# One encoder trunk on one core: the low part of each weight slab in four pieces

## The chip, the cores and the metric

The kernel runs on one core of a Trainium2 chip. A core has five engines with instruction queues of their own that meet through semaphores: TensorE (PE in the profile; its weight loads are shown as PEld), VectorE (DVE), ScalarE (ACT), GpSimd (POOL) and SyncE (SP), which here issues all DMA loads and stores. An engine takes its instructions in the order of its queue; one that waits holds up all behind it. The metric is the device time of one execution in microseconds, the median of several runs.

## The reference

The program is a hybrid encoder trunk of two layers over 1024 tokens and 1024 channels in float32. Each layer normalizes, modulates with shift and scale vectors that come from a conditioning vector, mixes, and adds the gated result to the stream:

```python
mod = c_act @ ada_w[l] + ada_b[l]
shift, scale, gate = jnp.split(mod, 3, axis=-1)
h = rms_norm(x, norm_g[l]) * (1.0 + scale[:, None, :]) + shift[:, None, :]
x = x + gate[:, None, :] * mixer(h)          # after both layers: rms_norm(x, final_g)
```

Layer 0's mixer projects `h @ w_in` into differential attention (4 heads, two softmax maps each) and a bidirectional gated linear recurrence, multiplies each by a SiLU gate and projects the pair with `w_out`. Layer 1's mixer is neighbourhood attention (16 heads on a 16 x 64 grid of tokens, 8 x 16 windows) with a SiLU gate, between two projections of the same kind.

## The kernel before

**Projections.** Activations stand channels by tokens in SBUF, split into eight row chunks of 128 channels (`KC = 8`) and two halves of 512 tokens (`HF`). Each projection works by weight slabs: a slab is 1024 input channels by 128 output channels, held as a tile of 128 partitions by 8 chunks by 128 columns. There are 80 slabs in one list: 24 of layer 0's input projection, 16 of its output projection (the same 8, once for each half of the tokens), 32 of layer 1's input and 8 of its output projection.

**Two-part products.** TensorE multiplies in a reduced float format (`F32R`). To keep float32 accuracy, every operand is split into a high part (the value rounded to that format) and a low part (the value minus the high part), and `mm3` (lines 203 to 206) issues three products for each chunk: high by high, high by the activation's low part, and the weight's low part by high. `proj` (line 245) runs the eight chunks of one slab over one half of the tokens, so 24 products into one PSUM bank; the low part of chunk k is first read by the third product of chunk k. In the value projection of layer 1 (`v1_job`) one slab holds four chunks of 256 columns.

**The supply of slabs.** `load_next` (line 152) issues the load of a raw slab (0.5 MB) on SP into one of two raw buffers. `split_next` (line 161) takes the next raw slab, lets ScalarE copy it into the high tile (line 187) and GpSimd subtract it into the low tile (line 188), and then issues the loads that may follow. A raw buffer is free for its next load when the slab's high and low parts are made; a high or low buffer is free when TensorE has read it. `ahead(i)` has a slab split while the one before is in use.

**What sets the order.** The kernel is recorded through a tile framework that tracks every tile's readers and writers, draws all semaphores, and orders each engine's queue itself by priorities and its own estimate of when things are ready; `high_priority` and `issue_after` bend that order in places. The two lines of the split are inside such a block.

**Stages.** At the start (0 to some 72 us) the first three slabs are multiplied chunk by chunk as the normalized activations come in (`products`, lines 573 to 575), while four groups of modulation sums (`mod_first`, line 281) arrive. Then come the recurrence (its scans and products on VectorE, `pair` and `evac_gb`, lines 743 to 822, with a small split of its own in `gate_w`, line 740), layer 0's attention (lines 982 to 1093; `head_norm` works by small dependent steps in `rstd_rows`, lines 388 to 394, on VectorE), the two output projections with layer 1's modulation sums woven in (`out_layer`, from line 1126; line 1160 sums squares for the next norm), layer 1's input projections and attention (`na_a`, `na_b`, `na_c`, lines 1360 to 1431; GpSimd scales the softmax rows at line 1389), and the last projection with the final norm.

Of the kernel before, what the change touches and what calls it, by code (L numbers as in the profile page):

```python
# [15 lines left out]
ALU = mybir.AluOpType  # L16
# [6 lines left out]
KC = 8  # L23
# [74 lines left out]
def kernel(ctx, tc, xT, xTp, small, lamp, adaw, tb, w0, gw, wo0, w1, nab, wo1, out):  # L98
    nc = tc.nc
    V, A, G, T = nc.vector, nc.scalar, nc.gpsimd, nc.tensor  # L100
# [51 lines left out]
    def load_next():  # L152
        i = state["load"]
        if i >= len(slabs):
            state["load"] = i + 1
            return
        raws[i] = wp.tile([P, KC, P], F32, tag="raw", name=f"raw{i}")
        nc.sync.dma_start(raws[i][:], slabs[i])
        state["load"] = i + 1

    def split_next():
        i = state["split"]
        if i >= len(slabs):
            return
        while state["load"] <= i:
            load_next()
        raw = raws.pop(i)
        pool = wp
        if state["third"] is not None:
            state["turn"] = (state["turn"] + 1) % 3  # L170
            pool = wp if state["turn"] else state["third"]
        tags = ("whi", "wlo")
        if i == 2:
            pool, tags = kqp, ("ks1", "ks1")
        if i == at1["g", 0]:
            pool, tags = mixp[1], ("mix6", "mix7")
        j = i - len(slabs) + KC
        if j >= 0:

            pool = (wp, kqp, mixa, mixp[1])[j // 2]  # L180
            if j >= 2:
                tags = (("ks0", "ks0"), ("ks1", "ks1"), ("mix0", "mix1"), ("mix2", "mix3"),
                        ("mix4", "mix5"), ("mix6", "mix7"))[j - 2]
        hi = pool.tile([P, KC, P], F32R, tag=tags[0], name=f"whi{i}")
        lo = pool.tile([P, KC, P], F32R, tag=tags[1], name=f"wlo{i}")
        with tc.high_priority() if j < 2 else tc.issue_after(state["pool"]):
            A.activation(hi[:], raw[:], AF.Copy)  # L187
            G.tensor_tensor(lo[:], raw[:], hi[:], ALU.subtract)  # L188
        ready[i] = (hi, lo)
        state["split"] = i + 1  # L190
        while state["load"] <= i + state["depth"]:
            load_next()

    def slab(i):
        while state["split"] <= i:
            split_next()
        return ready[i]

    def ahead(i):
        if state["split"] <= i:  # L200
            split_next()
# [423 lines left out]
    def evac_k(key):  # L625
        def f(hf, ps):
            if hf == 0 or (key, 0) not in ks_:
                ks_[key, 0] = kqp.tile([P, S], F32R, tag="ks0", name="ks0")
                ks_[key, 1] = kqp.tile([P, S], F32R, tag="ks1", name="ks1")
            def dst(t, b):  # L630
                x = t[b:b + 64, hf * HF:(hf + 1) * HF]
                return x if key[0] == "a" else by_tile(x)

            def src(b):
                x = ps[b:b + 64, :]
                return x if key[0] == "a" else x.rearrange("p (b g y) -> p b g y", g=2, b=4)

            k0, k1 = ks_[key, 0], ks_[key, 1]
            A.activation(dst(k0, 0), src(0), AF.Copy)
            A.activation(dst(k1, 64), src(64), AF.Copy)  # L640
            V.tensor_tensor(dst(k0, 64), src(0), dst(k0, 0), ALU.subtract)
            V.tensor_tensor(dst(k1, 0), src(64), dst(k1, 64), ALU.subtract)
        return f
# [261 lines left out]
    with ExitStack() as l0:  # L905
# [39 lines left out]
        for h in range(1, DA_HEADS):  # L945
            k = at0[c_k + h], evac_k(("a", h))
# [635 lines left out]
```

## Time and profile before

| | |
|---|---|
| three runs | 1188.19 us median (1186.65, 1188.19, 1191.43) |
| the profiled execution | 1190.72 us, span of its instructions 1189.0 us |
| busy: TensorE, VectorE, ScalarE, GpSimd | 1145.3, 738.1, 560.3, 371.8 us |
| the low parts (line 188) | 80 instructions, 197.0 us, 2465 ns each in the mean |
| the high parts (line 187) | 80 instructions, 84.3 us, 1056 ns each |
| TensorE's granted clock, mean | 0.989 |

The profile is one execution. Its page gives busy times, groups of instructions by source line, and for each group the idle time of the engine just ahead of it with what ended that idle time. Further views of the same trace are the waits by who waited for whom, a timeline of each engine (start, duration, line, operation, out<-in, and in brackets an idle time ahead and its releaser), statistics by line, and windows. Rows of "SPq" are DMA issues in SP's queue. A row with x2 or more merges instructions that follow each other. The durations on GpSimd are rougher than the others.

### The profile page before, as it was taken

To read this page: it belongs to the slowest core of one execution; us is meant where nothing else is said; L and a number is where in the kernel's file an instruction comes from. 1 tells how busy PE (TensorE), PEld (TensorE's weight loads), DVE (VectorE), ACT (ScalarE), POOL (GpSimd) and SP (SyncE) were. 2 spreads that over 40 slices of the span, in tenths; PEclk is the share of its full clock that TensorE was granted. 3 is DMA by queue.
4 is the path that set the end of the run, shared out by engine and by line. 5 is a ranking of instruction groups with operands and counts; after the bars stand their busy time and mean duration, and the time that the engine had idled before them with its cause. 6 is when DMAs were issued, how large, how long until landed. Compare 5 with 4: busy or idle time off the path is not lost.

```text
span 1189.0 us, 19211 instructions
## 1 busy us (share of the span) xinstructions
PE 1145.3 (96%) x7232; PEld 975.3 (82%) x7232; DVE 738.1 (62%) x1422; ACT 560.3 (47%) x1029; POOL 371.8 (31%) x346
## 2 busy tenths in 40 slices
PE   5999999999999999999999999999999999999997
PEld 2788777888887888777878888988998998888896
DVE  6857959699888979778663344233434443555454
ACT  4357685475655657432442444344444434446121
POOL 2124322233333332343422433332333333316100
PEclk8999999999999999999999999999999999999998
DMA  9723131432122112485513433243453534314212
GB/s 325 240 80 125 36 140 53 142 90 78 36 87 63 32 39 71 145 283 183 185 46 123 139 111 91 85 134 110 129 172 88 162 126 117 93 35 156 98 72 71
DMA packets 85789, 136.46 MB, mean 115 GB/s; under 512 B 8000, under 2 KB 49472, under 8 KB 85696
## 3 DMA queue, kind: packets, MB, share of 16 engines
q1 hardware_dynamic: 85696, 135.23, 36.3%
q8 instruction: 57, 0.93, 0.3%
q14 instruction: 36, 0.29, 0.1%
HBM read 112.13 MB, written 16.78 MB: 108 GB/s over the span
## 4 chain that ended last, share of the span: by engine, by line
PE 74%; DVE 13%; ACT 5%; DMA 4%; issue 3%; POOL 1%; SPq 0%; DVEq 0%; POOLq 0%; ACTq 0%
PE pp L204 14%; PE pp L205 14%; PE pp L206 14%; PE no L1418 4%; PE etr L1400 3%; PE v L204 2%; PE v L206 2%; PE v L205 2%; PE n L671 2%; DVE e L1003 2%; PE atr L1033 2%; PE n L672 2%; PE s L671 1%; PE s L672 1%; DMA ada<-in_adaw_dram 1%
## 5 line engine op out<-in xcount | busy, mean ns | idle before, releaser
L204 PE MATMUL pp<-ahi,whi 128*128 128x512 f32 (+1 forms) x976 | 370.8, 380 | 2.0 <-DVE sgb L677 1.8
L206 PE MATMUL pp<-ahi,wlo 128*128 128x512 f32 (+1 forms) x976 | 367.9, 377 | 1.1 <-POOL wlo L188 1.1
L205 PE MATMUL pp<-alo,whi 128*128 128x512 f32 (+1 forms) x976 | 368.6, 378 | 0.0
L188 POOL TENSOR_TENSOR wlo<-raw,whi 128x1024 fp32r<-128x1024 f32 x80 | 197.0, 2465 | 260.9 <-ACT whi L187 242.2
L206 PEld LDWEIGHTS pp<-ahi,wlo 128*128 128x128 f32 x976 | 184.0, 189 | 35.5 <-POOL wlo L188 1.6
L204 PEld LDWEIGHTS pp<-ahi,whi 128*128 128x128 f32 x976 | 184.3, 189 | 34.8 <-DVE sgb L677 2.3
L205 PEld LDWEIGHTS pp<-alo,whi 128*128 128x128 f32 x976 | 184.3, 189 | 30.8 <-issue 0.2
L1389 POOL TENSOR_SCALAR e<-e,r 128x288 f32<-128x288 f32 (+1 forms) x128 | 71.2, 569 | 235.9 <-DVE r L1387 229.7
L187 ACT ACTIVATE whi<-raw 128x1024 fp32r<-128x1024 f32 x80 | 84.3, 1056 | 107.1 <-PE pp L205 52.7
L1007 ACT ACTIVATE e<-e,nm 128x1024 f32<-128x1024 f32 x64 | 73.6, 1151 | 46.6 <-DVE nm L1003 46.3
L1384 ACT ACTIVATE e<-e,nm 128x288 f32<-128x288 f32 (+1 forms) x128 | 72.7, 569 | 47.2 <-DVE nm L1381 40.4
L1406 DVE COPY e<-etr 96x384 f32<-96x384 f32 (+1 forms) x64 | 35.5, 554 | 94.2 <-PE etr L1400 91.5
L1381 DVE CUSTOM_DVE_ANT_0 e<-n,bias 128x288 f32<-128x288 f32 (+1 forms) x128 | 60.6, 504 | 45.5 <-PE n L672 33.0
L1404 ACT ACTIVATE e<-etr 96x384 f32<-96x384 f32 (+1 forms) x64 | 31.3, 489 | 117.8 <-DVE e L1406 117.4
L1003 DVE CUSTOM_DVE_ANT_0 e<-s,tb 128x1024 f32<-128x1024 f32 x64 | 77.3, 1218 | 6.4 <-PE s L672 4.9
L1024 POOL TENSOR_SCALAR e<-e,r 128x256 f32<-128x256 f32 x32 | 32.6, 1018 | 131.8 <-DVE r L1013 73.7
L204 PE MATMUL v<-whi,ahi 128*128 128x256 f32 x256 | 72.2, 282 | 0.0
L206 PE MATMUL v<-whi,alo 128*128 128x256 f32 x256 | 71.9, 281 | 0.0
L205 PE MATMUL v<-wlo,ahi 128*128 128x256 f32 x256 | 71.9, 281 | 0.0
L1040 ACT ACTIVATE ath<-atr 128x512 fp32r<-128x512 f32 x64 | 37.5, 596 | 39.7 <-PE atr L1033 39.4
L1400 PE MATMUL etr<-ident,e 128*96 128x128 f32 (+1 forms) x384 | 52.3, 272 | 0.5 <-POOL e L1389 0.5
L671 PE MATMUL s<-ks,qq 128*128 128x512 f32 x128 | 52.5, 410 | 0.0
(218 smaller groups left out, 2111.3 us busy)
## 6 DMA issues: line engine op xcount, KB each, us to landing
raw<-in_w_dram SPq DMA_DIRECT2D x56, 512.0 KB
ada<-in_adaw_dram SPq DMA_DIRECT2D x96, 256.0 KB
raw<-in_wo_dram SPq DMA_DIRECT2D x24, 512.0 KB
bias<-in_nab_dram SPq DMA_DIRECT2D x64, 144.0 KB
qq<-qq SPq DMA_DIRECT2D x48, 128.0 KB
bias<-in_nab_dram SPq DMA_DIRECT2D x32, 192.0 KB
xT<-in_xT_dram SPq DMA_DIRECT2D x16, 256.0 KB
vd<-vt SPq DMA_DIRECT2D x32, 128.0 KB
```

What stands on the lines that cost most here:

```text
L187: A.activation(hi[:], raw[:], AF.Copy)
L188: G.tensor_tensor(lo[:], raw[:], hi[:], ALU.subtract)
L204: T.matmul(ps, lh, rh, start=start, stop=False)
L205: T.matmul(ps, lh, rl, start=False, stop=False)
L206: state["pe"] = T.matmul(ps, ll, rh, start=False, stop=stop).ins
L671: T.matmul(dst, qsel(q[m]), k, start=True, stop=False)
L1003: state["dve"] = V.tensor_tensor_reduce(out=e[:], in0=ps[:].rearrange("p a b -> p (a b)"), in1=tbt["tb"][:, o:o + S], scale=-1.0, scalar=3 ...
L1007: A.activation(e[:], e[:], AF.Exp, scale=-1.0, bias=nm[:], accum_out=sums[:, m:m + 1])
L1381: state["dve"] = V.tensor_tensor_reduce(out=e[:, m, :n], in0=ps[:, m, :n], in1=bias["now"][m][:, :n], scale=-1.0, scalar=3.0e38, op0=ALU.a ...
L1384: A.activation(e[:, m, :n], e[:, m, :n], AF.Exp, scale=-1.0, bias=nm[:, m:m + 1], accum_out=sums[:, m:m + 1])
L1389: state["pool"] = G.tensor_scalar(e[:, m, :n], e[:, m, :n], r[:, m:m + 1], 0.0, ALU.mult, ALU.add).ins
L1400: T.transpose(pt[:kn, m, j * P:(j + 1) * P], e[:, m, j * kn:(j + 1) * kn], ident[:])
```

## The change

The subtraction of line 188 is made by four instructions of two row chunks (256 columns) each instead of one of 1024 columns:

```diff
         with tc.high_priority() if j < 2 else tc.issue_after(state["pool"]):
             A.activation(hi[:], raw[:], AF.Copy)
-            G.tensor_tensor(lo[:], raw[:], hi[:], ALU.subtract)
+
+            for k in range(0, KC, 2):
+                G.tensor_tensor(lo[:, k:k + 2], raw[:, k:k + 2], hi[:, k:k + 2], ALU.subtract)
```

The high part stays one instruction on ScalarE, the loads stay whole slabs. Lines behind the change have numbers that are two higher in the changed program: the four pieces are line 190 there, `mm3`'s products 206 to 208.

GpSimd's queue at the end of layer 0, before and then with the change (`wlo40` is the low part of slab 40, the first of layer 1; `whi` the high part, `raw` the loaded slab):

```order
L188 TENSOR_TENSOR wlo40_5641<-raw40_5560,whi40_5640 128x1024
L188 TENSOR_TENSOR wlo42_5703<-raw42_5644,whi42_5702 128x1024
L188 TENSOR_TENSOR wlo41_5647<-raw41_5608,whi41_5646 128x1024
L188 TENSOR_TENSOR wlo43_5886<-raw43_5650,whi43_5885 128x1024
L188 TENSOR_TENSOR wlo44_5920<-raw44_5706,whi44_5919 128x1024
L188 TENSOR_TENSOR wlo45_6033<-raw45_5889,whi45_6032 128x1024
```

```order
L190 TENSOR_TENSOR wlo40_5761<-raw40_5677,whi40_5760 128x256 x4
L190 TENSOR_TENSOR wlo42_5829<-raw42_5767,whi42_5828 128x256 x4
L190 TENSOR_TENSOR wlo41_5770<-raw41_5728,whi41_5769 128x256 x4
L190 TENSOR_TENSOR wlo43_6015<-raw43_5776,whi43_6014 128x256 x4
L190 TENSOR_TENSOR wlo44_6052<-raw44_5835,whi44_6051 128x256 x4
L190 TENSOR_TENSOR wlo45_6168<-raw45_6021,whi45_6167 128x256 x4
```

The order of the slabs is kept (42 ahead of 41 in both), and the four pieces of a slab follow each other. Only in two slabs of the 80 something else of GpSimd's stands between the first piece and the other three: a memset of 64x512 in one, a step of a constant in the other.

TensorE's queue where slab 41 is first used, with the semaphores that each product waits for, before and then with the change (`ahi0` and `alo0` are the activation's parts of chunk 0):

```order
L204 MATMUL pp41_0_5708<-ahi0_0_5418,whi41_5646 128x512 [waits Activation_49]
L205 MATMUL pp41_0_5708<-alo0_0_5419,whi41_5646 128x512
L206 MATMUL pp41_0_5708<-ahi0_0_5418,wlo41_5647 128x512 [waits Pool_49]
L204 MATMUL pp41_0_5708<-ahi1_0_5423,whi41_5646 128x512
L205 MATMUL pp41_0_5708<-alo1_0_5424,whi41_5646 128x512
L206 MATMUL pp41_0_5708<-ahi1_0_5423,wlo41_5647 128x512
L204 MATMUL pp41_0_5708<-ahi2_0_5466,whi41_5646 128x512
L205 MATMUL pp41_0_5708<-alo2_0_5467,whi41_5646 128x512
L206 MATMUL pp41_0_5708<-ahi2_0_5466,wlo41_5647 128x512
```

```order
L206 MATMUL pp41_0_5837<-ahi0_0_5526,whi41_5769 128x512 [waits Activation_49]
L207 MATMUL pp41_0_5837<-alo0_0_5527,whi41_5769 128x512
L208 MATMUL pp41_0_5837<-ahi0_0_5526,wlo41_5770 128x512 [waits Pool_49]
L206 MATMUL pp41_0_5837<-ahi1_0_5531,whi41_5769 128x512
L207 MATMUL pp41_0_5837<-alo1_0_5532,whi41_5769 128x512
L208 MATMUL pp41_0_5837<-ahi1_0_5531,wlo41_5770 128x512
L206 MATMUL pp41_0_5837<-ahi2_0_5577,whi41_5769 128x512
L207 MATMUL pp41_0_5837<-alo2_0_5578,whi41_5769 128x512
L208 MATMUL pp41_0_5837<-ahi2_0_5577,wlo41_5770 128x512 [waits Pool_49]
```

The products stand in the same order. Before, the first product with the low part waits for the whole of it; now it waits for the piece of chunks 0 and 1, and the product of chunk 2 waits for the next piece. Over the program TensorE has 264 instructions that wait for GpSimd instead of 203.

TensorE's queue at the start, around the third group of modulation sums (`mod_500` before, `mod_509` with the change; `start` are the banks of the first three slabs):

```order
L575 MATMUL start_450<-alo_0_626,whi_295 128x512
L573 MATMUL start_669<-ahi_1_490,whi_464 128x512
L575 MATMUL start_556<-alo_1_491,whi_295 128x512
L573 MATMUL start_556<-ahi_1_495,whi_295 128x512
L574 MATMUL start_556<-ahi_1_495,wlo_296 128x512
L575 MATMUL start_556<-alo_1_496,whi_295 128x512
L281 MATMUL mod_500<-ada,c_126 32x128 x32
L575 MATMUL start_457<-alo_1_491,whi_388 128x512
```

```order
L575 MATMUL start_463<-ahi_1_499,whi_391 128x512
L283 MATMUL mod_509<-ada,c_126 32x128 x32
L577 MATMUL start_565<-alo_1_500,whi_295 128x512
L575 MATMUL start_565<-ahi_1_504,whi_295 128x512
L576 MATMUL start_565<-ahi_1_504,wlo_296 128x512
L308 MATMUL mod_509<-pick,mrow 128x4
L577 MATMUL start_565<-alo_1_505,whi_295 128x512
L576 MATMUL start_463<-ahi_1_499,wlo_392 128x512
```

The sums of the third group stand seven products earlier, those of the fourth likewise; a few steps of VectorE and ScalarE that belong to these groups move by one to three places. Behind the start the queues of TensorE, VectorE, ScalarE and SP are the same instruction by instruction.

## The prediction

> **What bounds the kernel now.** I read the page first: TensorE is the busy engine, and the instruction that the change cuts is GpSimd's largest group.
>
> ```profile
> PE 1145.3 (96%) x7232; PEld 975.3 (82%) x7232; DVE 738.1 (62%) x1422; ACT 560.3 (47%) x1029; POOL 371.8 (31%) x346
> L188 POOL TENSOR_TENSOR wlo<-raw,whi 128x1024 fp32r<-128x1024 f32 x80 | 197.0, 2465 | 260.9 <-ACT whi L187 242.2
> ```
>
> TensorE is idle for 1189.0 - 1145.3 = 43.7 us of the span; GpSimd works for 31% of it. So the time moves only where one of TensorE's few waits moves. The waits of TensorE by releaser are therefore the next view (us in total, times, longest).
>
> ```profile
> PE start L573 <- ACT ahi L415: 4.0, 2, 2.0
> PE obc L407 <- DVE osq L394: 2.3, 2, 2.0
> PE o L204 <- DVE atl L1041: 2.0, 2, 1.6
> PE n L671 <- DVE sg L677: 1.9, 1, 1.9
> PE pp L204 <- DVE sgb L677: 1.8, 1, 1.8
> PE pp L206 <- POOL wlo L188: 1.1, 1, 1.1
> ```
>
> In 80 slabs TensorE waits once for a low part, and for 1.1 us. The obvious gain, a first piece that is there early, is worth about that much. The other rows say where else to look: most of them end with VectorE. The statistics by line (min/median/max, ns) show that VectorE has something to do with the low parts:
>
> ```profile
> L188 POOL TENSOR_TENSOR wlo<-raw,whi x80: 2342/2402/3216, 6.4 to 1103.8; 128x1024 fp32r<-128x1024 f32 x80
> L1025 POOL TENSOR_TENSOR e<-e,e x32: 724/738/1387, 235.0 to 488.6; 128x256 f32<-128x256 f32 x32
> L1160 DVE TENSOR_TENSOR sq<-sq x34: 417/686/2765, 512.0 to 1175.9; 128x512 f32<-128x512 f32 x21, 128x256 f32<-128x256 f32 x13
> ```
>
> L1160, a sum of two SBUF tiles, takes 0.69 us in the median and up to 2.77. The timelines of layer 0's end show when (start, duration; `SPq` rows are DMA issues):
>
> ```profile
> 582.37 2.40 POOL L188 TENSOR_TENSOR wlo<-raw,whi 128x1024 fp32r<-128x1024 f32 x1 [3.03 <-ACT whi L187]
> 587.80 2.40 POOL L188 TENSOR_TENSOR wlo<-raw,whi 128x1024 fp32r<-128x1024 f32 x1 [3.04 <-ACT whi L187]
> 594.93 5.17 POOL L188 TENSOR_TENSOR wlo<-raw,whi 128x1024 fp32r<-128x1024 f32 x2 [4.73 <-ACT whi L187]
> ...
> 588.29 2.46 DVE L1160 TENSOR_TENSOR sq<-sq 128x512 f32<-128x512 f32 x1 [0.70 <-ACT sq L1154]
> 596.36 1.52 DVE L1160 TENSOR_TENSOR sq<-sq 128x512 f32<-128x512 f32 x1 [3.32 <-ACT sq L1154]
> ...
> 590.23 0.33 SPq L158 DMA_DIRECT2D raw<-in_w_dram  x1
> ...
> 593.79 2.01 ACT L187 ACTIVATE whi<-raw 128x1024 fp32r<-128x1024 f32 x2 [5.53 <-DMA raw<-in_w_dram]
> ```
>
> The sum that starts at 588.29 ends at 590.75, 0.55 us after the low part's end at 590.20: VectorE stands still while GpSimd's instruction runs. The pair at 594.93 shows who is next: the first low part ends about 597.33, the sum of 596.36 ends at 597.88, again 0.55 us later, though GpSimd's second instruction was already queued; and the pair takes 5.17 instead of 2 x 2.40 = 4.80, so the second one waited for VectorE. They alternate, one instruction each. This is what four pieces change.
>
> **The change, part by part.**
>
> *What GpSimd pays.* A two-input piece of 256 columns has a row of its own, L1025: 0.74 us. Four make 2.95 us, 0.55 more than 2.40, alone; 80 x 0.55 = 44 us on an engine with 1189.0 - 371.8 = 817 us idle, so nothing by itself. Below: the pieces stream with no cost each, 2.40; above: 4 x 1.387 = 5.5 us, the longest row. I take 0.55, since nearly all L1025 rows stand at the median. [...]
>
> *What VectorE gains.* An operation with two SBUF inputs that meets a low part now waits for one piece, at most 0.74 us, not for up to 2.4. But with four pieces queued, up to four of VectorE's operations in a row each wait for one: a dense run of them loses as much as before, only spread. A gain is left where fewer than four stand in the way. So I go to TensorE's waits one by one, with 0.74 us for each wait.
>
> A, the start:
>
> ```profile
> 21.88 2.81 POOL L188 TENSOR_TENSOR wlo<-raw,whi 128x1024 fp32r<-128x1024 f32 x1 [12.37 <-ACT whi L187]
> 21.72 3.52 DVE L414 SCALAR_TENSOR_TENSOR xT<-xT,gain,bcs 128x512 f32<-128x512 f32 x2
> ```
>
> Two operations of about 0.7 us take 3.52: about 2.1 us of waiting. With pieces the second ends about 1.4 us earlier; the next ones (L416, L535) then pay for the other pieces. Bounds -1.4 and +0.6 us (three more waits); I take -1.0, as TensorE waits for the first of them.
>
> B, layer 0's second group of gates (TensorE's 1.8 us wait for `sgb`):
>
> ```profile
> 200.40 2.69 POOL L188 TENSOR_TENSOR wlo<-raw,whi 128x1024 fp32r<-128x1024 f32 x1 [9.46 <-ACT whi L187]
> 200.93 3.24 DVE L798 TENSOR_TENSOR t<-t,w 128x1024 f32<-128x1024 f32 x1
> 204.09 0.68 DVE L677 SCALAR_TENSOR_TENSOR sgb<-sgb,pp 128x512 f32<-128x512 f32 x1
> ```
>
> One operation in the way, then L677, which takes its second input from PSUM. L798 is held for about 2.69 + 200.40 - 200.93 = 2.16 us; a piece holds it for 0.74: -1.4, and I take -1.5 of the 1.8 there (bounds 0 and -1.8).
>
> C, the head norm (TensorE's longest `osq` wait, 2.0 us):
>
> ```profile
> 374.66 2.79 POOL L188 TENSOR_TENSOR wlo<-raw,whi 128x1024 fp32r<-128x1024 f32 x1 [6.54 <-PE s L672]
> 375.13 2.47 DVE L394 SCALAR_TENSOR_TENSOR osq<-osq 128x128 f32<-128x128 f32 x1
> 378.29 0.29 DVE L394 SCALAR_TENSOR_TENSOR osq<-osq 128x128 f32<-128x128 f32 x1
> 378.60:383.00 4.40, 4.37 (x18) 4.10 (x19) 2.84 (x6) 0.60 (x1) 2.44 (x3) 0.61 0.45 140
> ```
>
> Here four small dependent operations follow each other (L394, L392, L393, L394), so each may meet a piece: 4 x 0.74 = 3.0 against 2.47 - 0.29 = 2.2 us now. If a piece only holds VectorE for the 0.55 us seen above, 2.2 as well, less what the first has already run. Bounds -0.7 and +0.8; I take -0.3.
>
> D, two gate products before the last head:
>
> ```profile
> 476.68 3.50 DVE L943 TENSOR_TENSOR vT<-vT,sga 128x512 f32<-128x512 f32 x2
> 480.10 1.28 DVE L1041 TENSOR_TENSOR atl<-atr,ath 128x512 fp32r<-128x512 f32 x2
> ```
>
> Two operations of 0.7 us take 3.50; with a wait of 0.74 each, 2.9: L1041, for which TensorE waits 1.6 us, comes 0.6 to 1.1 us earlier. I take -0.9.
>
> *What the finer wait gains.* F: the one wait of TensorE for a low part (1.1 us) is for the second of the pair at 594.93. Its first piece alone is wanted, but the chain in front of it gets longer: low part 587.80 (+0.55, and one wait of 0.55 for L1160), then the load that may only be issued when it has ended (590.23), then the copy on ScalarE (593.79), then the four pieces of the other slab. So: the last low part costs 0.74 where it cost 2.40 and 0.37 of waiting (5.17 - 4.80), -2.0; the chain ahead of it +0.55 + 0.55, and the other slab's pieces +0.55. That is -0.4 us; bounds -1.1 and +1.0.
>
> *What it costs.* G: a slab's raw buffer is free, and its next load issued from SP's queue, only when the last piece is done. This is covered nearly everywhere, but not at the entry to layer 1's attention:
>
> ```profile
> 622.30 4.76 POOL L188 TENSOR_TENSOR wlo<-raw,whi 128x1024 fp32r<-128x1024 f32 x2 [22.20 <-ACT whi L187]
> 624.73 0.33 SPq L158 DMA_DIRECT2D raw<-in_w_dram  x1
> 629.03 1.06 ACT L187 ACTIVATE whi<-raw 128x1024 fp32r<-128x1024 f32 x1 [3.53 <-DMA raw<-in_w_dram]
> 630.12 0.60 ACT L676 ACTIVATE sg<-pp 128x512 f32<-128x512 f32 x1
> 632.97 1.37 SPq L1357 DMA_DIRECT2D bias<-in_nab_dram  x3
> 641.21 0.56 DVE L1381 CUSTOM_DVE_ANT_0 e<-n,bias 128x384 f32<-128x384 f32 x1 [2.80 <-DMA bias<-in_nab_dram]
> 641.83 0.44 PE L671 MATMUL n<-ks,qq 128*128 128x384 f32 x1 [1.05 <-DVE nm L1381]
> ```
>
> The low part that starts at 622.30 frees the load of 624.73; its landing ends ScalarE's wait at 629.03; L676 is queued behind that copy, VectorE's `sg` behind L676, and TensorE's 1.9 us wait ends there. +0.55. The next low part, later by as much and longer by as much, holds SP's next weight load, and the bias loads at 632.97 are queued behind that; TensorE's 1.05 us wait at 641.83 ends with a bias: +0.55 again. Together +1.1 (bounds 0 and +2).
>
> *At nothing.* The 61 waits that TensorE gains for single pieces end long before it comes to them, apart from F. The sums of two modulation groups move seven matmuls forward on TensorE at the start; the same matmuls run, and if the loads are not there yet the wait is inside A's bounds. The memset that now stands behind the first piece of C's slab gives VectorE one more opening there, inside C's bounds.
>
> Sum: -1.0 - 1.5 - 0.3 - 0.9 - 0.4 + 1.1 = **-3.0 us**. The profiled execution took 1190.72 us (span 1189.0), so about 1187.7; the median of the three runs is 1188.19, 2.5 lower, and on it I forecast **1185.2 us**: 0.3% less, which is no change that can be measured. 0.5% is 5.9 us, about what a measurement of this kernel can tell.
>
> **The rivals.**
>
> *More comes back (faster).* The window quoted under C has a granted clock of 0.61 in the 4.4 us after that wait: 4.4 x 0.39 = 1.7 us lost besides the wait itself. If the wait shrinks and the clock stays up, if pieces hold VectorE for 0.55 rather than 0.74 (A -1.4, B -1.8, C -0.7, D -1.1) and if G is hidden, the sum is -1.4 - 1.8 - 0.7 - 1.7 - 1.1 - 1.1 = -7.8: **1180.4**. For it: the 0.55 was seen twice. Against: C has four operations in a row, and G's waits are real. [...]
>
> *Nothing but G (no change).* If GpSimd keeps its turn from piece to piece, VectorE waits as before and 0.55 us longer: +1.1, **1189.3**. The pair at 594.93 speaks against it, but those were two instructions with different waits, not four with none between them.
>
> *The supply runs late (slower).* Place: the out projection and layer 1's first slabs (about 500 to 600 us), where the low parts of 582.37 and 587.80 stand 5.43 us apart, so two raw buffers must turn round in 10.9. A slow load there takes
>
> ```profile
> 524.99 6.54 DMA raw<-in_wo_dram
> ```
>
> 6.54; with the copy (1.06) and the low part (2.40) that makes 10.0, and 0.9 is left. It decides from a low part of 3.3 us on, and 2.95 plus one wait of 0.55 for L1160 is 3.5. Then each of some seven turns costs 0.2 us or more, and each new TensorE wait can drop the clock as under C (1.7 us): 7 x 0.2 + 4 x 1.7 + G 1.1 = +9.3, **1197.5**. Against: most loads there take 3.5 us (590.23 to the copy at 593.79), and TensorE waits for no slab there ahead of the one at F.
>
> **How the numbers follow.** The forecast (-3.0, its own range 1182 to 1188) 0.46; more comes back 0.24; nothing but G 0.20; supply late 0.10. Low: 1180, the faster rival's number. High: 1191, that of the rival without a gain, with the 1.5 us by which the median stands above the fastest run. That leaves out the slower case and the fast half of the faster one. Faster by over 0.5% (below 1182.3): 0.24 from the one rival and 0.02 from the forecast's edge; slower (above 1194.1): 0.10; the rest, 0.64, is no change.
>
> **What would show it.** Right: GpSimd's line has 320 operations of about 0.74 us and busy time grows by some 45 us; L1160's longest falls from 2.77 to below 1.6; TensorE's waits for `sgb` near 204 and `o` near 480 shrink by about 1 us, those near 631 and 641 grow by 0.5 each. Wrong: VectorE's longest waits stay at 2.4 and more (GpSimd keeps its turn); pieces of 0.9 us and more; new TensorE waits on `wlo` or on `whi` between 500 and 600 (supply); a changed share of slow clock, which would outweigh the sum.

## The result and the profile after

The changed kernel took **1180.93 us** in the median of seven runs (1179.38 to 1184.22), the kernel before 1188.19 (1185.11 to 1191.43, seven runs): a ratio of 0.9942, 95% interval 0.9924 to 0.9959. Set against it again beside the last experiments, it came to 0.9958 (0.9946 to 0.9970). So it is faster by about half a per cent, 5 to 7 us; 3.0 us were forecast. The profiled execution took 1183.27 us (span 1181.5), 7.45 less than the one before.

The page after, engines and the group of the low parts:

```profile
PE 1142.2 (97%) x7232; PEld 974.7 (82%) x7232; DVE 715.9 (61%) x1422; ACT 559.5 (47%) x1029; POOL 440.5 (37%) x586
L190 POOL TENSOR_TENSOR wlo<-raw,whi 128x256 fp32r<-128x256 f32 x320 | 264.3, 859 | 221.0 <-ACT whi L187 199.0
```

GpSimd works 69 us more, VectorE 22 us less: the instructions of VectorE that stood still behind a low part stand still for less. TensorE's waits after (us in total, times, longest):

```profile
PE start L575 <- ACT ahi L417: 4.5, 2, 2.5
PE n L673 <- DVE sg L679: 2.8, 1, 2.8
PE obc L409 <- DVE osq L396: 1.3, 2, 0.8
PE o L206 <- DVE atl L1043: 0.9, 2, 0.6
```

The 1.8 us for `sgb` in `pp` are gone, the longest `osq` wait fell from 2.0 to 0.8, `atl` from 1.6 to 0.6; the wait for `sg` grew from 1.9 to 2.8. Two stretches of the trace say more than these totals.

**Behind slab 29, in the out projection.** Timeline before (GpSimd's low part of slab 29, VectorE, SP's issues, ScalarE, TensorE):

```profile
520.23 2.62 POOL L188 TENSOR_TENSOR wlo<-raw,whi 128x1024 fp32r<-128x1024 f32 x1 [4.48 <-ACT whi L187]
520.63 2.77 DVE L344 SCALAR_TENSOR_TENSOR macc<-ada,ctmp,macc 128x512 f32<-128x512 f32 x1
524.09 0.33 SPq L1152 DMA_DIRECT2D x1d<-xh  x1
524.46 0.44 SPq L330 DMA_DIRECT2D ada<-in_adaw_dram  x1
524.99 0.40 SPq L158 DMA_DIRECT2D raw<-in_wo_dram  x1
531.64 1.06 ACT L187 ACTIVATE whi<-raw 128x1024 fp32r<-128x1024 f32 x1 [4.86 <-DMA raw<-in_wo_dram]
532.91 0.59 PE L361 MATMUL mrow<-pick,macc 128*128 128x4 f32 x2 [2.75 <-ACT macc L356]
```

and the same in the timeline after:

```profile
514.85 3.39 POOL L190 TENSOR_TENSOR wlo<-raw,whi 128x256 fp32r<-128x256 f32 x4 [2.08 <-ACT whi L187]
514.34 1.90 DVE L346 SCALAR_TENSOR_TENSOR macc<-ada,ctmp,macc 128x512 f32<-128x512 f32 x2
518.27 0.33 SPq L158 DMA_DIRECT2D raw<-in_wo_dram  x1
525.08 1.06 ACT L187 ACTIVATE whi<-raw 128x1024 fp32r<-128x1024 f32 x1 [2.99 <-DMA raw<-in_wo_dram]
526.36 0.38 PE L363 MATMUL mrow<-pick,macc 128*128 128x4 f32 x2 [0.61 <-ACT macc L358]
```

What SP's queue waits for in this stretch, before (519.3 to 527 us) and then after (513 to 519), of the latter the wait of the load itself:

```profile
SPq L1152 <- DVE xh L1149: 3.2, 1, 3.2
```

```profile
SPq L158 <- POOL wlo L190: 0.4, 1, 0.4
```

Before, slab 29's low part holds the `macc` sum for 2 us; `xh` behind it is late, and the load of slab 31 stands in SP's queue behind the store of `xh`, which waits 3.2 us, and a load of `ada`. The raw buffer is free when slab 29's low part ends, at 522.85; the load goes out at 524.99, 2.14 us later. After, the low part ends at 518.24 and the load goes out at 518.27: nothing but the low part holds it. ScalarE's copy waits for the load; the small `macc` copy on which TensorE waits stands behind it in ScalarE's queue. Two windows, before and then after, show what came next (length; busy PE, PEld, DVE, ACT, POOL; granted clock, DMA share, GB/s):

```profile
533.00:539.00 6.00, 6.00 (x15) 4.80 (x16) 3.14 (x4) 0.38 (x1) 2.14 (x1) 0.50 1.01 376
```

```profile
526.00:532.00 6.00, 5.64 (x26) 4.72 (x27) 3.99 (x5) 1.47 (x4) 3.45 (x4) 1.00 0.91 311
```

With the 2.75 us wait came 6.83 us at half clock (532.27 to 539.09 in the trace's clock record): 15 products in 6 us against 26. No term of the prediction's sum stands for this place.

**The entry to layer 1's attention**, timeline after (SP's issue, ScalarE, TensorE):

```profile
615.41 0.33 SPq L158 DMA_DIRECT2D raw<-in_w_dram  x1
620.10 1.06 ACT L187 ACTIVATE whi<-raw 128x1024 fp32r<-128x1024 f32 x1 [4.35 <-DMA raw<-in_w_dram]
622.55 0.44 PE L673 MATMUL n<-ks,qq 128*128 128x384 f32 x1 [2.81 <-DVE sg L679]
```

The load of slab 45 is issued 4.33 us ahead of the start of TensorE's wait (622.55 - 2.81 - 615.41); before it was 4.85 (631.49 - 1.91 - 624.73). That is the 0.5 us by which slab 43's low part ends later. And the clock is half for 3.41 us behind the longer wait (623.11 to 626.52).

TensorE's progress puts the parts together: how much earlier (-) the same product starts than in the trace before, in us, at the times of that trace, with four of the experiments below. The first column holds the start, where the clock is half for 6.83 us in the trace before and for 13.65 in the one after.

```
time before        96    168    216    340    407    469    497    521    551    601    624    862   span
the change       +0.8   +0.6   -1.6   -1.6   -3.9   -3.3   -4.4   -4.4   -9.4   -9.9   -9.8   -7.5   -7.5
the change again +0.8   +0.6   -1.5   -1.5   -3.9   -3.4   -4.5   -4.5  -10.3  -10.4  -10.4   -8.3   -7.4
e1_four_slabs    +1.4   +1.4   -0.2   -0.2   -2.2   -2.2   -3.3   -3.3   -8.6   -8.6   -8.6   -7.0   -7.9
e2_all_but_four  +0.7   +0.5   -0.2   -0.2   -2.3   -1.7   -1.7   -1.7   -6.2   -6.6   -6.6   -4.3   -4.2
e4_slab29        -0.2   -0.2   +1.4   +1.4   +0.3   +0.3   +0.3   +0.3   -5.5   -5.5   -5.5   -2.9   -2.9
e12_low43        +1.5   +1.3   -0.9   -0.9   -3.6   -3.0   -4.1   -4.1  -10.0  -10.4  -10.4  -12.5  -13.2
```

### The profile page after: what moved, and what is told of

The parts are those of the page before. It is cut to its first block, busy times and chain, and to the rows that moved or that the text cites. A ratio compares the mean times of both kernels' runs of the same rounds, so it can differ in the third digit from the quotient of the medians.

```text
span 1181.5 us, 19490 instructions
## 1 busy us (share of the span) xinstructions
PE 1142.2 (97%) x7232; PEld 974.7 (82%) x7232; DVE 715.9 (61%) x1422; ACT 559.5 (47%) x1029; POOL 440.5 (37%) x586
## 4 chain that ended last, share of the span: by engine, by line
PE 76%; DVE 9%; DMA 6%; ACT 4%; POOL 2%; issue 1%; SPq 0%; DVEq 0%; ACTq 0%; POOLq 0%
PE pp L206 15%; PE pp L207 15%; PE pp L208 15%; PE no L1420 4%; PE etr L1402 3%; PE v L206 2%; PE v L208 2%; PE v L207 2%; POOL wlo L190 2%; PE atr L1035 2%; PE n L673 2%; DMA ada<-in_adaw_dram 2%; DVE e L1005 2%; PE n L674 2%; PE s L673 1%
## 5 line engine op out<-in xcount | busy, mean ns | idle before, releaser
L190 POOL TENSOR_TENSOR wlo<-raw,whi 128x256 fp32r<-128x256 f32 x320 | 264.3, 859 | 221.0 <-ACT whi L187 199.0
L1009 ACT ACTIVATE e<-e,nm 128x1024 f32<-128x1024 f32 x64 | 73.6, 1150 | 46.6 <-DVE nm L1005 46.3
L1151 DVE SCALAR_TENSOR_TENSOR xh<-pp,mod,xh 128x512 f32<-128x512 f32 (+1 forms) x37 | 23.4, 634 | 49.9 <-PE pp L208 43.3
```

The costliest lines, as they stand in the source:

```text
L190: G.tensor_tensor(lo[:, k:k + 2], raw[:, k:k + 2], hi[:, k:k + 2], ALU.subtract)
L1009: A.activation(e[:], e[:], AF.Exp, scale=-1.0, bias=nm[:], accum_out=sums[:, m:m + 1])
```

## The experiments

Theory: the gain sits in four places (slabs 13, 21, 24, 29) where one long low part held a VectorE operation on whose successors TensorE or SP's queue waited (B, C and D of the prediction, and the place behind slab 29). Rivals: the finer wait of TensorE for single pieces, or shorter holds all over the program. Line numbers are those of the changed kernel; "whole" means one operation of 1024 columns. Each ratio is against the kernel before, on the same chip.

**The four slabs alone (`e1_four_slabs`), and all but these (`e2_all_but_four`).**

```diff
-            for k in range(0, KC, 2):
-                G.tensor_tensor(lo[:, k:k + 2], raw[:, k:k + 2], hi[:, k:k + 2], ALU.subtract)
+            for k in range(0, KC, (w := 2 if i in (13, 21, 24, 29) else KC)):
+                G.tensor_tensor(lo[:, k:k + w], raw[:, k:k + w], hi[:, k:k + w], ALU.subtract)
```

> Pieces in slabs 13, 21, 24 and 29 alone, one operation in the other 76. Theory (the gain sits in four places where one long low part held a VectorE operation that TensorE, or SP's queue, was waiting for): TensorE's progress in the two traces gives -1.6 us at slab 13, -2.1 at slab 21 (with the clock), -1.1 at slab 24 and -5.0 behind slab 29, -9.8 together, and neither the +1.2 of the start nor the +2.4 at the entry to layer 1's attention: about 1178.4. Rival (the finer wait of TensorE for single pieces, or shorter holds all over the program): four slabs of 80 bring at most a few tenths, about 1187.5.

Measured: 1181.91 us, 0.9928 (0.9908 to 0.9949): 7.1 us less than the kernel before beside it (1189.00), of the 9.8 that the theory expected. Four slabs of 80 bring what the change brings, not more. TensorE's waits show what is back and what isn't:

```profile
PE start L575 <- ACT ahi L417: 6.1, 2, 4.1
PE n L673 <- DVE sg L679: 2.0, 1, 2.0
PE pp L208 <- POOL wlo L190: 1.1, 1, 1.1
PE obc L409 <- DVE osq L396: 1.0, 2, 0.7
```

The wait for a low part is back at 1.1 us, and the sum is no worse for it. The start, which is instruction for instruction that of before, has one wait of 4.1 us in place of 2.0: it varies from run to run.

With the condition turned round (whole in the four, pieces in the other 76):

> Pieces in all slabs but 13, 21, 24 and 29. Theory of the four places: their waits stay as they were before the change (1.85 us near 204, 1.98 near 378, 1.64 near 480, 2.75 near 532 with 6.8 us of half clock behind it), the costs stay: +1.2 + 2.4 = about 1191.8, not faster than before. Rival (finer wait, or shorter holds everywhere): nearly the whole gain of the change, 1181 to 1182.

Measured: 1186.50 us, 0.9971 (0.9956 to 0.9986): by the ratios half to two thirds of the gain of the change, outside both expectations. Its waits:

```profile
PE obc L409 <- DVE osq L396: 2.6, 2, 2.0
PE o L206 <- DVE atl L1043: 2.0, 2, 1.7
PE mrow L363 <- ACT macc L358: 1.2, 1, 1.2
PE pp L206 <- DVE sgb L679: 1.1, 1, 1.1
```

At slabs 21 and 24 the waits are as before the change; `mrow` (2.75 before) and `sgb` (1.85) are partly gone. Near 204, VectorE's L800 starts 0.25 us earlier and TensorE itself comes 0.5 later than before. Behind slab 29 the traces of these kernels compare as follows (us; the lead is from the issue of slab 31's load to the start of TensorE's `mrow` wait, or to where it would start):

```
                  load behind the end of slab 29's low part    lead    mrow wait
before                            2.14                         5.17      2.75
e2_all_but_four                   2.13                         6.41      1.17
e4_slab29                         0.03                         6.41      0.0
the change                        0.03                         7.48      0.61
```

The whole low part holds the load in `e2_all_but_four` as it did before; the pieces in other slabs bring the supply 1.2 us further ahead of TensorE, by which step is not shown. So the four slabs are enough for the gain, but they don't hold all of it, and the gains of the two halves don't add up to that of the change.

**Slab 29 alone** (`e4_slab29`: `2 if i == 29 else KC`).

> Pieces in slab 29 alone. Theory: VectorE's macc (L346) and then its xh (L1151) are held 0.55 instead of 2.2 us, SP's store of xh is issued earlier and with it slab 31's load behind it; TensorE's wait for mrow near 532 falls from 2.75 to below 0.9, and the 6.8 us at half clock behind it do not come: -5.0, about 1183.2. Rival (the wait shrinks, the clock halves all the same): -2, about 1186. Rival (the load of slab 31 is late for another reason, such as the slab's own length): no change, 1188.

Measured: 1187.10 us, 0.9978 (0.9962 to 0.9994): 2 to 3 us, where the theory expected 5.0. At its place the trace shows what the theory said: TensorE's `mrow` wait is gone, the clock stays up there, and TensorE gains 5.8 us on before (the table, 521 to 551). Timeline:

```profile
520.16 1.89 DVE L346 SCALAR_TENSOR_TENSOR macc<-ada,ctmp,macc 128x512 f32<-128x512 f32 x2
524.07 0.33 SPq L158 DMA_DIRECT2D raw<-in_wo_dram  x1
529.05 1.06 ACT L187 ACTIVATE whi<-raw 128x1024 fp32r<-128x1024 f32 x1 [2.90 <-PE pp L208]
```

Two `macc` sums take 1.89, and ScalarE's copy now waits for a buffer that TensorE frees, not for the load. But in this execution two other waits, which the edit doesn't touch, were followed by slow clock where the profiled execution before had none: 1.8 us for `sgb` near 204 and 3.0 us for `sg` near 627 (granted clock in the windows behind them, 0.57 and 0.51):

```profile
205.30:208.70 3.40, 3.40 (x10) 2.63 (x10) 2.47 (x3) 1.23 (x2) 0.00 (x0) 0.57 0.43 159
628.00:631.50 3.50, 3.50 (x19) 3.50 (x18) 0.00 (x0) 0.00 (x0) 0.20 (x1) 0.51 0.63 200
```

And the place has no fixed price: `e10_start_only`, below, has its wait too, with 3.41 us of half clock behind it and not 6.83. So a pair of profiles doesn't tell what one place brings to the median; the 5.8 us are what this pair of executions shows, and 2 to 3 is what the median shows.

**Pieces in reverse order** (`e3_reversed`).

```diff
-            for k in range(0, KC, 2):
+            for k in range(KC - 2, -1, -2):
```

> Four pieces as in the change, in reverse order, so that the piece of chunks 0 and 1, which TensorE wants first, is made last. VectorE is held by one piece as in the change; TensorE has no earlier first piece than the end of the whole low part. Theory: the gain of the change stays but for the one wait for a low part near 590 (three pieces of 0.74 later: +2.2 at most, and less where the next waits take it in): 1180.9 to 1183.1; TensorE's queue at the start also has the order from before the change, worth up to -1.2. Rival (the finer wait is what gains): back to 1188.

Measured: 1186.68 us, 0.9974 (0.9959 to 0.9989), outside both expectations. The waits that end with VectorE are as with the change (`osq` 0.8 at the longest, no `sgb`, no `mrow`), so the shorter holds don't depend on which piece comes first. What is lost stands in TensorE's timeline where slab 41 is first used:

```profile
592.09 0.80 PE L208 MATMUL pp<-ahi,wlo 128*128 128x512 f32 x1 [2.29 <-POOL wlo L190]
```

and in the window around it:

```profile
590.00:597.00 7.00, 4.91 (x12) 3.86 (x13) 4.46 (x12) 0.00 (x0) 2.04 (x3) 0.55 0.46 150
```

2.29 us of waiting where the change has 0.19, and half clock from 590.65 to 597.48. TensorE works in it from 592.09 on: 2.1 + 5.4/2 = 4.8 us; by TensorE's progress in the two traces, 4.6. In the time it is 5.75 us to the change by the medians, 2 to 4 by the ratios. The wait I had counted; the clock I had not. By the time alone this lies nearer to the rival; but `e1_four_slabs` has the whole gain with one whole low part at slab 41, so the finer wait is not what gains. It is worth having with pieces, though not as a gain over the whole operation (1.1 us of waiting there): it keeps the four pieces, which end later, from costing more.

**Pieces at the start alone** (`e10_start_only`: `2 if i < 3 else KC`; it has the change's order of TensorE's start).

> Pieces in slabs 0, 1 and 2 alone (with the changed order of two modulation groups on TensorE that this brings). Theory that the start is no part of the gain, since the two kernels whose programs are equal there came through it 1.6 us apart: within 1 us of before, 1188 to 1190. Rival (step A of the prediction: VectorE is released sooner there): -1.0, and with a shorter slow clock up to -3, 1186 to 1188. Rival (TensorE's third product came 1.2 us later in the changed kernel's profile because of the pieces): +1.2, 1190.

Measured: 1188.43 us, 1.0002 (0.9986 to 1.0018). The start brings and costs nothing that the runs can tell (-1.7 to +2.1 us). The trace also repeats the place behind slab 29 as it was before, `mrow` wait and slow clock included (TensorE's waits):

```profile
PE mrow L363 <- ACT macc L358: 2.5, 1, 2.5
```

**Two pieces (`e5_two`), and eight (`e6_eight`)**: `range(0, KC, 4)` and `range(0, KC, 1)`, with pieces of as many chunks as the step.

> Two pieces of four row chunks instead of four of two. A piece then takes about 1.27 us (0.137 + 2.26/2 by the two sizes measured, 2.40 for 1024 columns and 0.70 for 256), and holds a VectorE operation for about 1.1 instead of 2.2 (whole) or 0.55 (four pieces). Theory: the waits near 204, 378, 480 and 532 come out between, about 0.8, 1.4, 1.1 and 1.6 us, all below those that halved the clock: 1182 to 1184.5. Rival (what counts is only that VectorE gets a turn at all between pieces): as the change, 1181. Rival (one long operation behind another is needed to hold VectorE that long, so two pieces hold it as whole ones do): 1187 to 1189.

Measured: 1181.97 us, 0.9954 (0.9938 to 0.9970): most of the gain. VectorE at slab 13 and at slab 24:

```profile
199.55 2.14 DVE L800 TENSOR_TENSOR t<-t,w 128x1024 f32<-128x1024 f32 x1
472.19 3.49 DVE L945 TENSOR_TENSOR vT<-vT,sga 128x512 f32<-128x512 f32 x2
```

L800 took 3.24 us behind a whole low part, 2.14 here, 1.60 with four pieces (200.80 in the trace after): with about 1.08 of its own it is held for 2.16, 1.06 and 0.52. The two products of L945, of 0.68 us each where nothing holds them, took 3.50 (whole), 3.49 (two pieces), 2.40 (four): held for 2.1, 2.1 and 1.0 us together. By an estimate from these, a whole one holds only the first, two pieces hold both for half as long each (1.06), four hold both for a quarter each (0.52). The waits for `osq` (1.8) and `atl` (1.6) stay accordingly, against the expected 1.4 and 1.1; those for `sgb` and `mrow` are gone, and with `mrow` its slow clock.

> Eight pieces of one row chunk. A piece then takes about 0.42 us, eight 3.4 instead of 2.8. Theory: VectorE's operations are held less each (0.3 instead of 0.55) but by more pieces in a row, so the four places gain a few tenths at most over the change; the load of slab 45 is issued another 0.5 us later, and the wait at the entry to layer 1's attention grows by that: 1181 to 1182.5. Rival (finer is better): 1179 or less. Rival (GpSimd falls behind where VectorE alternates with it, and the supply runs late between 500 and 600): 1184 or more, with new waits for whi or wlo there.

Measured: 1194.18 us, 1.0047 (1.0027 to 1.0067): slower than before. The third expectation, that GpSimd falls behind where VectorE alternates with it, came true, but at another place: in layer 0's recurrence. GpSimd's timeline there:

```profile
131.43 12.60 POOL L190 TENSOR_TENSOR wlo<-raw,whi 128x128 fp32r<-128x128 f32 x8 [8.01 <-ACT whi L187]
```

TensorE's waits:

```profile
PE n L673 <- DVE sg L679: 3.2, 1, 3.2
PE gate L208 <- POOL gwl L742: 2.7, 1, 2.7
PE no L1420 <- ACT e L1406: 1.8, 1, 1.8
```

At their median of 0.46 us, eight pieces make 3.7 us together. Between 131 and 144 they take 12.6, since VectorE's operations there, most of them of 1.3 to 2.5 us, go between them. Slabs 8 and 9, with another split between them, hold GpSimd until 155, the small split `gwl` behind them comes late, and TensorE waits 2.7 us for it (0.6 with the change); slow clock follows, there and at the two other waits above. By TensorE's progress this place is 3.7 of the 11.4 us by which this trace stands behind that of the change; the rest is spread over later places.

**Pieces in slabs 3 to 42** (`e8_3_42`: `2 if 3 <= i < 43 else KC`).

> Pieces in slabs 3 to 42, one operation in the start's three slabs and from slab 43 on. Theory: all four places as in the change, and the one wait for a low part near 600; the load of slab 45's raw data at the entry to layer 1's attention is issued 4.85 us ahead of TensorE's wait again and not 4.33, so that wait is 0.5 shorter, and below 2.3 us, where the clock halved in every profile so far: 0.5 to 2 us less than the change, 1179 to 1180.5. Rival (the pieces after slab 42 bring something too): 1181 to 1183.

Measured: 1181.93 us, 0.9940 (0.9917 to 0.9963). The wait for `sg` is 2.0 us, with no slow clock behind it in this execution, as expected; but the 0.5 to 2 us that the theory expected from this are not in the median, which shows no difference to the change.

**The stores from ScalarE's queue**, alone (`e9_store_act`) and with pieces in slabs 3 to 42 (`e11_store_and_pieces`).

```diff
-                        nc.sync.dma_start(xdst[c * P:(c + 1) * P, hf * HF:(hf + 1) * HF], x)
+                        nc.scalar.dma_start(xdst[c * P:(c + 1) * P, hf * HF:(hf + 1) * HF], x)
```

> No pieces at all (one operation of 1024 columns in all slabs, as before the change); only the stores of layer 0's output (L1154) are issued from ScalarE's queue, ahead of the square that reads the same tile, and no longer from SP's. It is asked how the held VectorE operation behind slab 29 reached the load of slab 31: through the store that stood ahead of it in SP's queue and waited for xh, or through the loads of ada, which wait for VectorE's macc and stand there too (with the edit three of them stand ahead of that load instead of one). Theory (store): the load is issued 4.7 us or more ahead of the sums (L380) that precede TensorE's mrow wait, against 3.6 before, and the wait falls from 2.75 (2.55 in another run of the same program there) below 1.7. Rival (ada): the load stays where it was or is later, and the wait stays at 2.5 or more. Time 1185 to 1189 by the first, 1188 to 1191 by the second.

Measured: 1188.85 us, 1.0006 (0.9992 to 1.0020). Timeline of SP's issues and of TensorE:

```profile
525.73 0.33 SPq L332 DMA_DIRECT2D ada<-in_adaw_dram  x1
526.15 0.38 SPq L158 DMA_DIRECT2D raw<-in_wo_dram  x1
533.01 0.39 PE L363 MATMUL mrow<-pick,macc 128*128 128x4 f32 x2 [1.78 <-ACT macc L358]
```

Inconclusive. Without the store in front of it, the load is issued 3.5 us ahead of the sums, as before (3.6), now right behind a load of `ada`; the wait is 1.8 us, because the load itself was quicker (5.6 instead of 6.65 us to the copy). What that `ada` waited for (SP's queue, 521 to 527):

```profile
SPq L332 <- DMA x1d<-xe: 4.0, 1, 4.0
```

It waits, by the profile, for the landing of one of the moved stores. So the edit put a wait of its own in the place of the one that it took away. In the trace before, the store of `xh` is what waited; whether `ada` would have held the load without it stays open.

> Pieces in slabs 3 to 42 and the stores of layer 0's output from ScalarE's queue, as a candidate. If the store in SP's queue still costs something: 1 us under pieces in 3 to 42 alone, 1180 to 1181. Rival (with the pieces SP's queue holds nothing that TensorE waits for): no change to those, 1181 to 1182.5.

Measured: 1183.40 us, 0.9969 (0.9955 to 0.9982), above both expectations: no gain over pieces alone. The load of slab 31 goes out 0.8 us behind slab 29's low part again, and SP's queue has the same kind of wait for a moved store (3.9 us).

**Slab 43's low part on VectorE** (`e12_low43_on_vector`).

```diff
-            for k in range(0, KC, 2):
-                G.tensor_tensor(lo[:, k:k + 2], raw[:, k:k + 2], hi[:, k:k + 2], ALU.subtract)
+            for k in range(0, KC, (w := 2 if 3 <= i < 43 else KC)):
+                (V if i == 43 else G).tensor_tensor(lo[:, k:k + w], raw[:, k:k + w], hi[:, k:k + w], ALU.subtract)
```

> Pieces in slabs 3 to 42, and the low part of slab 43 made by VectorE in one operation (some 1.4 us, by 0.69 for 512 columns of L1162) instead of GpSimd. Theory of the entry to layer 1's attention (the load of slab 45 waits for slab 43's low part, and everything up to TensorE's wait for sg stands behind that load): the load is issued about 1 us earlier, the wait falls from 2.0 (2.8 with the change) to about 1.0, and no slow clock follows it: 1179 to 1180.5. Rival (the load's own time, 4.3 to 5.4 us in the runs so far, or the rotary products that VectorE makes behind it, decide): no gain, 1181 to 1182.5.

Measured: **1176.86 us, 0.9908 (0.9895 to 0.9921)**. That is below both expectations, in four runs. Timeline at the entry to layer 1's attention, and then, of TensorE's waits, the one for `sg`:

```profile
611.95 1.23 DVE L190 TENSOR_TENSOR wlo<-raw,whi 128x1024 fp32r<-128x1024 f32 x1 [2.13 <-ACT whi L187]
613.21 0.33 SPq L158 DMA_DIRECT2D raw<-in_w_dram  x1
616.90 1.06 ACT L187 ACTIVATE whi<-raw 128x1024 fp32r<-128x1024 f32 x1 [1.69 <-DMA raw<-in_w_dram]
```

```profile
PE n L673 <- DVE sg L679: 0.2, 1, 0.2
```

1.23 us on VectorE instead of 2.4 on GpSimd: the load goes out 6.0 us ahead of where TensorE's wait stood (4.33 with the change), and ScalarE's copy starts 3.7 us after it (4.7 with the change). The wait for `sg` falls to 0.2 us, and the slow clock is gone. 1.7 us of this are the edit's; the 1.0 us by which the load was quicker may be chance. Between 601 and 862 this is 4.2 us against the changed kernel (the table: -10.4 to -12.5, against -10.4 to -8.3).

The changed kernel beside it (`after_again`):

> The changed kernel once more, on the chip of these runs, to set the candidates against it: 1180 to 1182, and a wait for sg of 2.3 us or more at the entry to layer 1's attention with a slow clock behind it.

Measured: 1182.25 us, 0.9958 (0.9946 to 0.9970). The same wait of `n`:

```profile
PE n L673 <- DVE sg L679: 2.9, 1, 2.9
```

The two intervals lie apart: the version with slab 43 on VectorE beats both kernels. It has whole low parts at the start and behind slab 43 as well, as `e8_3_42` has; the interval of that one, on another chip, just touches (from 0.9917). How much of the gain slab 43 alone brings is therefore less sure than that the version is faster.

## Why the prediction was right in part

The direction was right, and the median lies in the range, at its low end: 1180.93 against 1185.2, a gain of 7.3 us (4.8 in the second comparison) for 3.0. That it lies there is in part luck: the range's low end was the faster rival's number, and the largest gain in the traces had no term in the sum. Whether the 0.64 for a change of less than 0.5% were too much stays open: the two comparisons give 0.58% and 0.42%.

*The cost of a piece.* Forecast 0.74 each, 0.55 more per slab. Undisturbed, four take 2.83 us in a row (0.71 each), 0.43 more than 2.40, or 34 us for 80 slabs. The busy time grew by 69, not 45 us: the rest stands where the pieces alternate with VectorE (slab 12: 8.06 us).

*What VectorE gains.* Right in mechanism: it gets its turn after each piece, L1162's longest is 1.26 us (2.77 before). A hold is about 0.5 (0.4 to 0.55), not 0.74, as one rival had it.

*A, the start, -1.0.* Not there. The two `xT` operations take 2.36 instead of 3.52, and the next ones pay for it (L418 2.37 instead of 1.62), as the step's other bound had it. Pieces at the start alone change nothing that the runs can tell.

*B, `sgb`, -1.5.* The wait is gone; TensorE gains 2.2 at that place in the trace.

*C, head norm, -0.3.* The step that failed by size within the sum: the count of operations that meet a piece. Four were assumed; two did, held 0.54 and 0.41 us (L396, 0.83 and 0.70 instead of 0.29). The wait fell by 1.2, beyond the lower bound of -0.7, and the slow clock behind it (3.41 us, 1.7 lost) did not come. In the pair of traces that is -2.3.

*D, gate products, -0.9.* -1.1 (3.50 to 2.40).

*F, -0.4.* The wait for a low part went from 1.1 to 0.2; TensorE gained 0.3 there.

*G, +1.1.* The 0.55 at slab 45's load was right (0.52). The second 0.55, for the bias, did not come (1.05 and 1.0 us). What was missed is the price of the longer wait: 2.8 us brought slow clock, 1.9 had not in the trace before. In the pair of traces the place costs 2.4. In `e4_slab29`, without any piece there, the wait was 3.0 as well, for the load took 5.4 us: over the traces with whole low parts there it is 1.9 to 3.0, so the pieces add 0.5 to a wait that varies by 1.

*What was left out: the load behind a store.* The largest term, -5.0 in the traces, had no line in the sum. L344's 2.77 us at 520.63 is the same pattern as B, and the load of 6.54 us that the rival "supply late" quotes is the very one that went out late. But I followed VectorE's held operations only where TensorE waits for VectorE. Here the wait is for ScalarE, four steps on: `macc` and `xh` on VectorE, SP's queue, a load, ScalarE's queue. The rival even put a loss there.

*The rivals.* "More comes back" (1180.4) came nearest, with two of its three grounds: the shorter hold and the clock. That G is hidden was wrong, and its number is right by luck: without the place that it left out too, it would have been some 5 us off by the pair of traces. The slow clock behind C did not come in the trace after, as it forecast; but behind a wait of 1.99 us at that place in `e2_all_but_four` it did not come either (last section). "Nothing but G" fell with the alternation. "Supply late" did not happen with four pieces; with eight a small split came late, through VectorE's turns and not through the loads.

## What to carry to other kernels

When an operation of one engine holds up another, follow each held operation through every queue to its end, DMA queues included, and not only to the engine that waits for it directly: the largest effect was three queues away. What cutting a blocking operation pays depends on what stands behind it: by an estimate from the holds measured here, n operations of the other engine in a row lose about min(n, pieces) times the hold of one piece, so two pieces brought nothing where two stood in a row (L945: 3.50 us whole, 3.49 with two, 2.40 with four). And each cut gave the other engine a turn too, at the price of its own operations (12.60 us for eight pieces between VectorE's): four pieces were right here (0.9942), eight were slower than one (1.0047). Then cut only where it is needed: four slabs of 80 gained as much as all 80.

## What the runs showed that was not expected

**Short waits of TensorE and its clock.** In the 14 profiles (those of the kernel before, of the changed kernel twice and of the 11 experiments), between 45 and 1150 us, TensorE waited 56 times for 1 us or more in one piece:

```
length of the wait    times    with slow clock behind it (granted 0.5 for 3.41 or 6.83 us)
1.03 to 1.67 us        27       0
1.77 to 2.02 us        15       7
2.20 to 3.22 us        14      13
```

Each of the 20 stretches of slow clock in that part of the program begins in such a wait or at most 1.6 us behind it. By half of its length, an estimate, one costs up to 1.7 or 3.4 us, as much as the wait itself or more, so in these traces what a wait is worth jumps near 2 us.

Whether it does goes, in these traces, with where the wait lies in time. All changes of the granted clock in one trace stand whole multiples of 3.41 us apart (to within 0.01 us in the traces before and after), on a grid that lies elsewhere in each execution. The same wait for `osq`, 1.98 us in the trace before and 1.99 in `e2_all_but_four`, shows what that does (two neighbouring cells of the grid from each, columns as above):

```profile
375.25:378.67 3.42, 1.44 (x8) 0.86 (x6) 3.30 (x5) 1.53 (x3) 2.72 (x2) 1.00 0.56 134
378.67:382.08 3.41, 3.41 (x14) 3.31 (x15) 1.88 (x4) 0.48 (x1) 1.95 (x3) 0.50 0.54 173
```

```profile
373.93:377.34 3.41, 1.93 (x9) 1.27 (x7) 3.34 (x4) 2.06 (x4) 3.25 (x2) 1.00 0.48 115
377.34:380.76 3.42, 2.92 (x19) 2.66 (x20) 3.29 (x8) 0.60 (x1) 2.36 (x3) 1.00 0.57 192
```

Before, the wait lies whole in one cell: TensorE is idle for 1.98 us of it, and the next cell runs at half clock. In the other a border of the grid cuts it into 1.48 and 0.50 us, and the clock stays up. So it goes over all 14 traces: each of the 20 stretches begins at the end of a cell with 1.78 us or more of idle time; of the cells with that much only two (1.83 and 1.85 us) had none behind them, and no cell with less (1.72 at most) had one. Why two of the stretches last two cells is not shown. This fits the spread of the kernel before (1184 to 1195 us in the runs beside the first experiments, with a mean granted clock of 0.994 in the fastest and 0.984 in the slowest) and is why a single profile doesn't tell a place's share of the median.

**Both engines pay for the alternation.** With four pieces, the low part of slab 12 took 8.06 us in the recurrence, where VectorE's operations are 1.2 to 2.3 us long, against 2.67 whole; it cost nothing there because no one waited for it. The engines took turns there, one instruction each: the four pieces ended at 189.29, 191.97, 194.65 and 196.33, VectorE's operations between them at 191.44, 194.12 and 195.73.
